# The last part of an encoder's output projection: row tile by row tile, with held-back matmuls, other buffers for its mixer, and another order in the first gates

## Chip, core and metric

The kernel runs on one core of one Trainium2 chip. The metric is the device time of one execution in microseconds (us), the median of several executions. The engines are named as the profile names them: PE is TensorE (matmuls; PEld is its weight load, which overlaps), DVE is VectorE, ACT is ScalarE, POOL is GpSimd, and SP (SyncE) issues the DMAs.

## What is computed

A two-layer encoder over one sequence of 512 tokens of width 1024, in float32. Each layer adds four attention mixers of four heads each (a: a neighbourhood on a grid, b: differential, c: dilated, d: with a latent key and value), projected back by `w_o`, and then a gated feed-forward block; a norm ends the program. Cut to what matters here:

```python
for l in range(DEPTH):
    h = rms_norm(x, attn_norm[l])
    ...
    mix = jnp.concatenate([o_a, o_b, o_c, o_d], axis=-1)
    x = x + mix @ w_o[l]

    h = rms_norm(x, ffn_norm[l])
    x = x + (jax.nn.silu(h @ w_gate[l]) * (h @ w_up[l])) @ w_down[l]
return rms_norm(x, final_norm)
```

## The kernel before

**Products.** Activations lie transposed: 128 channels on the partitions, the 512 tokens along the row. Every float32 operand of a large product is split into a hi part (a cast to fp32r) and a lo part (the rest), and a product is three matmuls, hi by hi, lo by hi and hi by lo. `dense_steps` (L166) writes them for one output tile of 128 by 512: for each of the inputs `k` the weight's hi part by the activation's hi part (L173) and by its lo part (L175), and after all of these the weight's lo part by the activation's hi part (L178). A weight slab of 1024 columns is loaded by SP, cast to hi on ACT (L137; `whi`, two buffers) and subtracted to lo on DVE or POOL (L160; `wlo`, two buffers).

**Order.** Each engine runs its instructions in program order. A scheduler in the framework fixes that order when the program is built, by priorities that follow the order of writing; `tc.issue_after(i)` lets what is written inside stand behind instruction `i`. Attention is written as 56 units of scores (`S_`), transposes (`T_`, tile `tp`) and the product with the values (`V_`, tile `pv`). Between the units, `fill` hands out pieces of dense work at hand-set rates: the input projections, and the output projection in three parts by mixer, `PARTS = ((1,), (2, 3), (0,))`. Part 0 adds mixer b, part 1 mixers c and d (four slabs of two row tiles, `wo1m`), part 2 mixer a (two slabs of four row tiles, `wo2m`). A piece starts when its `gate` is ready. Mixer a is the last to be computed, so part 2 ends the attention of each layer.

**Around the last unit.** `V_` of the last unit (L937) leaves mixer a's last head in the bank `pv`. `fold` copies one half to SBUF on ACT (L137, tile `o`) and adds the other on DVE (L781), and `split` casts the sum to the hi part of tile `mix01` on ACT (L137) and subtracts to its lo part on DVE (L142), each in two pieces. The same has been done for the first two heads (`mix00`). All mixer tiles come from one ring of four buffers, so the tiles of mixer a take those that mixer c's had. `p_out` adds each row tile to the residual `x` on DVE straight from PSUM (L663), or, where the table `ENG` says so (keys `x22`, `x23`, `x27` in part 2), by a copy on ACT (L655) and an add on POOL.

**Into the feed-forward block.** `norm_inputs` makes of each of the eight residual tiles the scaled hi part `h_f` on ACT (L200), the lo part on DVE (L201), and its square on ACT, which POOL adds up (L190, L191). The gate and up slabs of the feed-forward block (tile `gu`) follow, 22 pairs of 24 matmuls a slab, eight inputs in `dense` order.

**The end.** The last output tile is computed in two halves of 256 tokens. For each half a column of `ms` gives the factor `rcol_fin` (POOL), DVE multiplies it into a diagonal (L1154, `dg`), a matmul with ones spreads it over the partitions (L1156, `bc`), and four multiplications on DVE (L1159) and four DMAs end the program.

Of the kernel before, what the change touches and what calls it, by code (L numbers as in the profile page):

```python
# [18 lines left out]
P = 128  # L19
D = 1024  # L20
S = 512
# [17 lines left out]
NEED = {(3, 0, 0): [('out', 0, 1)], (0, 1, 1): [('out', 1, 3)]}  # L39
HEADS = [(1, 0, 0), (1, 0, 1), (1, 1, 0), (1, 1, 1), (2, 0, 0), (2, 0, 1), (2, 1, 0), (2, 1, 1), (3, 0, 0), (3, 0, 1), (3, 1, 0), (3, 1, 1), (0, 0, 0), (0, 0, 1), (0, 1, 0), (0, 1, 1)]  # L40
ORDER = 'f t s 1q1 v2 1k1 2q0 l0 2k0 2k1 l1 kr nq 2q1 nqr l2 nk nkr qr 3r00 3q0 v3 3k1 3q1 v00 3k0 v01 o01 0k0 3r01 3r10 3r11 vt1 0q1 ab 0q0 vt0 0k1 o00 o10 o11 o12 o13 o20 o21'
# [4 lines left out]
ENG = {'b10_l': 'P', 'b11_l': 'P', 'ea00': 'V', 'ea03': 'A', 'ea10': 'A', 'ea13': 'A', 'ec11': 'A', 'ec13': 'A', 'ed00': 'P', 'ed02': 'P', 'ed03': 'A', 'ed11': 'P', 'ed13': 'A', 'fa010': 'P', 'fa110': 'P', 'fa210': 'P', 'fa300': 'P', 'kd_a00': 'P', 'kd_a01': 'V', 'kd_a11': 'P', 'kd_d00': 'P', 'kd_d01': 'P', 'kd_d10': 'P', 'kd_d11': 'P', 'kl_a00': 'P', 'kl_a01': 'P', 'kl_a10': 'P', 'kl_a11': 'P', 'kl_c00': 'P', 'kl_c01': 'P', 'kl_c10': 'P', 'kl_c11': 'P', 'kl_d00': 'P', 'kl_d01': 'P', 'kl_d10': 'P', 'kl_d11': 'P', 'm10_l': 'P', 'm11_l': 'P', 'm20_l': 'P', 'm21_l': 'P', 'm30_l': 'P', 'm31_l': 'P', 'ql_a00': 'P', 'ql_a01': 'P', 'ql_a10': 'P', 'ql_a11': 'P', 'ql_c00': 'P', 'ql_c01': 'P', 'ql_c10': 'P', 'ql_c11': 'P', 'ql_d00': 'P', 'ql_d01': 'P', 'ql_d10': 'P', 'ql_d11': 'P', 'rk2': 'V', 'rq1': 'V', 'sc_ka0': 'P', 'sc_ka1': 'P', 'sc_qn1': 'P', 'wh_ckv': 'V', 'wh_cq0': 'P', 'wh_kb0': 'V', 'wh_qb0': 'V', 'wh_qb1': 'V', 'wh_ud1': 'V', 'wh_ur': 'V', 'wh_vcb': 'V', 'wh_wo00': 'P', 'wh_wo14': 'P', 'wl_qb1': 'V', 'x02': 'P', 'x03': 'P', 'x05': 'P', 'x15': 'P', 'x22': 'P', 'x23': 'P', 'x27': 'P'}  # L46
# [16 lines left out]
def tile_encoder(ctx, tc, xT, gains, lamv, w_in, w_kr, w_d, w_o0, w_o1, w_o2, w_gu, w_dn,  # L63
# [103 lines left out]
    def dense_steps(pt, w, xs, wcol, first=True, last=True):  # L167
# [3 lines left out]
        nk = len(xs)  # L171
        for k in range(nk):
# [20 lines left out]
    def norm_inputs(x, gcol, nm):  # L193
# [3 lines left out]
        for k in range(KD):  # L197
            h = wide(f"h_{nm}{k}", F32R)
            g = gn[:, gcol + k : gcol + k + 1]
            nc.scalar.activation(h[:, 0, :], x(k), AF.Copy, scale=g)  # L200
# [3 lines left out]
            square(acc, x(k), k, nm)  # L204
# [127 lines left out]
    def attention(l, xsrc, x, hs, ssq, pl, nar):  # L332
# [331 lines left out]


        mix = {}

        def mix_tile(m, p):
            if (m, p) not in mix:
                mix[m, p] = pl.tile([P, 2, S], F32R, tag="mix", name=f"mix{m}{p}_{l}", bufs=4)  # L670
            return mix[m, p]
# [649 lines left out]
```

## Time and profile before

| | |
|---|---|
| time, median of 3 executions | 1305.89 us (1305.41 to 1307.08) |
| the profiled execution's own time | 1306.79 us |
| its span, first to last instruction | 1305.0 us |
| PE busy | 1275.5 us, 98% of the span |
| DVE, ACT, POOL busy | 687.6, 588.8, 474.9 us |
| mean granted clock of PE over the span | 0.994 |

The profiled execution lies 0.90 us above the median; 1.8 us of its time lie outside the span. The granted clock is given as a share of 2.4 GHz: 1.00 is that level, 0.50 the lower one of 1.2 GHz, and a value between them is a stretch with some of both. A row of the view by stretches tells, for each engine, in the order PE, PEld, DVE, ACT, POOL, how long it was busy in the stretch and how many of its instructions lie in it (one on an edge may count on both sides). A matmul's record is longer than its share of PE's time, since one drains while the next runs; what it costs is the distance from its start to the next start.

### The profile page before, as it was taken

What the parts mean: (1) busy time and instruction counts of PE and PEld (TensorE: products, weight loads), DVE (VectorE), ACT (ScalarE), POOL (GpSimd) and SP (SyncE); (2) the same over time, 40 slices, a digit from 0 to 9 for tenths busy, and PEclk for the clock granted to TensorE, in tenths of its full rate; (3) what the DMA queues carried; (4) which work ended last, traced back from release to release, by engine and by line L of the source; (5) the groups of instructions that cost most, each with busy time, mean ns of one, the idle gap of its engine ahead of it and who ended that gap; (6) DMA issues with size and microseconds to landing.
All of it is one profiled execution on the core that took longest, in us unless ns stands there. A gap on an engine that the chain in (4) does not pass through costs nothing. (4 is left out here: it accounts for less than half of the span.)

```text
span 1305.0 us, 17103 instructions
## 1 busy us (share of the span) xinstructions
PE 1275.5 (98%) x6362; PEld 1067.1 (82%) x6362; DVE 687.6 (53%) x1168; ACT 588.8 (45%) x1022; POOL 474.9 (36%) x371
## 2 busy tenths in 40 slices
PE   8999999999999999999999999999899999999997
PEld 8788888877888888888898788888688888888886
DVE  6588756665444444323237787565654444442232
ACT  5376866753333333222316777676433333333230
POOL 1276685763111111100246469656521111110000
PEclk9999999989999999999999999999999999999998
DMA  5552441112222222333346333311222222233221
GB/s 191 175 166 85 134 118 65 67 64 97 97 97 97 97 97 93 101 118 107 122 129 176 111 103 111 122 65 66 75 87 97 97 97 97 97 93 101 89 89 65
DMA packets 50915, 135.63 MB, mean 104 GB/s; under 512 B 7896, under 2 KB 12760, under 8 KB 50832
## 3 DMA queue, kind: packets, MB, share of 16 engines
q1 hardware_dynamic: 50544, 134.25, 32.3%
q8 instruction: 50, 0.82, 0.3%
q10 hardware_dynamic: 288, 0.29, 0.1%
q14 instruction: 33, 0.27, 0.1%
HBM read 119.01 MB, written 4.23 MB: 94 GB/s over the span
## 5 line engine op out<-in xcount | busy, mean ns | idle before, releaser
L175 PE MATMUL gu<-h_f,whi_gu 128*128 128x512 f32 x704 | 274.3, 390 | 1.5 <-DVE h_f L201 1.5
L173 PE MATMUL gu<-h_f,whi_gu 128*128 128x512 f32 x704 | 274.0, 390 | 0.1
L1110 POOL TENSOR_TENSOR u<-u,th 128x512 f32<-128x512 f32 x44 | 93.2, 2118 | 367.6 <-DVE u L1108 351.5
L178 PE MATMUL gu<-h_f,wlo_gu 128*128 128x512 f32 x704 | 173.9, 389 | 0.0
L175 PEld LDWEIGHTS gu<-h_f,whi_gu 128*128 128x128 f32 x704 | 132.0, 188 | 31.0 <-DVE h_f L201 4.0
L173 PEld LDWEIGHTS gu<-h_f,whi_gu 128*128 128x128 f32 x704 | 132.2, 188 | 28.3 <-DVE x L663 1.0
L178 PEld LDWEIGHTS gu<-h_f,wlo_gu 128*128 128x128 f32 x704 | 132.1, 188 | 27.4
L137 ACT CAST whi_gu<-raw_gu 128x1024 fp32r<-128x1024 f32 x88 | 92.7, 1054 | 105.5 <-PE gu L175 104.9
L173 PE MATMUL dn<-act,whi_dn 128*128 128x512 f32 x330 | 128.4, 389 | 0.0
L175 PE MATMUL dn<-act,whi_dn 128*128 128x512 f32 x330 | 128.4, 389 | 0.0
L160 DVE TENSOR_TENSOR wlo_gu<-raw_gu,whi_gu 128x1024 fp32r<-128x1024 f32 x88 | 110.4, 1255 | 20.3 <-ACT whi_gu L137 18.7
L692 ACT ACTIVATE e<-e,mx 128x512 f32<-128x512 f32 (+1 forms) x128 | 85.5, 669 | 49.0 <-DVE mx L690 44.3
L160 DVE TENSOR_TENSOR wlo_dn<-raw_dn,whi_dn 128x1024 fp32r<-128x1024 f32 (+1 forms) x45 | 51.1, 1135 | 100.4 <-PE dn L178 61.0
L137 ACT CAST whi_dn<-raw_dn 128x1024 fp32r<-128x1024 f32 (+1 forms) x45 | 44.2, 982 | 127.7 <-PE dn L175 111.2
L137 ACT CAST act<-u 128x512 fp32r<-128x512 f32 x44 | 27.3, 620 | 155.1 <-POOL u L1110 155.1
L1108 DVE SCALAR_TENSOR_TENSOR u<-gu,bc_ff 128x512 f32<-128x512 f32 x44 | 30.4, 691 | 122.8 <-PE gu L178 122.8
L142 DVE TENSOR_TENSOR tl<-tp,th 128x512 fp32r<-128x512 f32 x112 | 75.6, 685 | 28.7 <-ACT th L137 28.0
L178 PE MATMUL dn<-act,wlo_dn 128*128 128x512 f32 x330 | 82.1, 389 | 0.0
L690 DVE CUSTOM_DVE_ANT_0 e<-sc,t 128x512 f32<-128x512 f32 x96 | 65.0, 684 | 32.3 <-PE tp L853 12.6
L178 PEld LDWEIGHTS dn<-act,wlo_dn 128*128 128x128 f32 x330 | 61.9, 188 | 12.9
L175 PEld LDWEIGHTS dn<-act,whi_dn 128*128 128x128 f32 x330 | 61.9, 188 | 12.9
L173 PEld LDWEIGHTS dn<-act,whi_dn 128*128 128x128 f32 x330 | 61.9, 188 | 12.8
(484 smaller groups left out, 2644.6 us busy)
## 6 DMA issues: line engine op xcount, KB each, us to landing
raw_gu<-in_w_gu_dram SPq DMA_DIRECT2D x88, 512.0 KB, 3.2
raw_dn<-in_w_dn_dram SPq DMA_DIRECT2D x32, 512.0 KB, 3.5
raw_wo<-in_w_o_dram SPq DMA_DIRECT2D x16, 512.0 KB, 3.5
t<-tb SPq DMA_DIRECT2D x16, 448.0 KB, 4.1
raw_dn<-in_w_dn_dram SPq DMA_DIRECT2D x16, 384.0 KB, 3.0
sb<-kbn SPq DMA_DIRECT2D x64, 64.0 KB, 2.0
sb<-qbn SPq DMA_DIRECT2D x64, 64.0 KB, 2.0
xin<-in_xT_dram SPq DMA_DIRECT2D x8, 256.0 KB, 5.6
```

What stands on the lines that cost most here:

```text
L137: nc.scalar.copy(out, src)
L142: engine(tag, usual).tensor_tensor(out, src, hi.bitcast(F32), op=ALU.subtract)
L160: lo_eng.tensor_tensor(lo[:, c], raw[:, c], hi[:, c].bitcast(F32), op=ALU.subtract)
L173: nc.tensor.matmul(pt, whi[:, k, wcol], xs[k][:, 0, :], start=first and k == 0, stop=False)
L175: nc.tensor.matmul(pt, whi[:, k, wcol], xs[k][:, 1, :], start=False, stop=False)
L178: nc.tensor.matmul(pt, wlo[:, k, wcol], xs[k][:, 0, :], start=False, stop=last and k == nk - 1)
L690: nc.vector.tensor_tensor_reduce(out=e, in0=sc, in1=bias, scale=1.0, scalar=BIG, op0=ALU.add, op1=ALU.min, accum_out=mx)
L692: nc.scalar.activation(e, src, AF.Exp, bias=mx, scale=-1.0, accum_out=den)
L1108: nc.vector.scalar_tensor_tensor(u, pts[1], 0.5, r_bc, op0=ALU.mult, op1=ALU.mult)
L1110: nc.gpsimd.tensor_tensor(u, u, th, op=ALU.mult)
```

## The change

- In part 1 the last slab (`wo16`, `wo17`) waits for a new mark, `last`, which the transposes of the last unit set; from then on `fill` places the work behind the last unit's `pv` matmuls, whose last one is now the unit's mark.
- Part 2 is one piece, `p_out_last`: both slabs are asked for at its start, its row tiles cycle through the four banks of `acc` and `sc`, each row tile does its six matmuls tile of the mixer by tile of the mixer (hi by hi, hi by lo, lo by hi), each row tile stands behind the one before, and every add to `x` is on DVE from PSUM. `ENG` loses its keys `x22`, `x23` and `x27`.
- The tiles of mixer a come from the ring `st` of ten buffers.
- `norm_inputs` of the feed-forward block writes the squares behind the last hi part.
- The first gate and up slab (`m == 0`) take all hi by hi matmuls first, then the weight's lo part, and the activation's lo part last.
- At the end two transposes of the factor's column (L1195) take the place of the diagonal and the matmul with ones.

```diff
-NEED = {(3, 0, 0): [('out', 0, 1)], (0, 1, 1): [('out', 1, 3)]}
+NEED = {(3, 0, 0): [('out', 0, 1)], (0, 1, 1): [('out', 1, 2)]}
...
+        if lo_last:
+            for i, (w, a) in enumerate(((whi, 0), (wlo, 0), (whi, 1))):
+                for k in range(nk):
+                    nc.tensor.matmul(pt, w[:, k, wcol], xs[k][:, a, :], start=first and i + k == 0,
+                                     stop=last and i == 2 and k == nk - 1)
+                    yield 1.0
+            return
...
-            square(acc, x(k), k, nm)
+            if not late:
+                square(acc, x(k), k, nm)
+        if late:
+            with tc.issue_after(last.ins):
+                for k in range(KD):
+                    square(acc, x(k), k, nm)
...
+        def p_out_last(part, kts):
+            xs = [mix[k] for k in kts]
+            ws = []
+            for i in range(2):
+                w = slab((w_o0, w_o1, w_o2)[part][l][:, i * SLAB : (i + 1) * SLAB], SLAB, nc.gpsimd, f"wo{part}{4 * i}{l}")
+                ws.append(tuple(t.rearrange("p (m k c) -> p m k c", m=4, k=2) for t in w))
+            last = None
+            for m in range(KD):
+                pt = ps.tile([P, 512], F32, tag=("acc", "sc")[m // 2 % 2], name=f"wo{part}{m}{l}", bufs=2)
+                with tc.issue_after(last.ins) if last else ExitStack():
+                    for k in range(2):
+                        whi, wlo = (t[:, m % 4, k] for t in ws[m // 4])
+                        nc.tensor.matmul(pt, whi, xs[k][:, 0, :], start=k == 0, stop=False)
+                        nc.tensor.matmul(pt, whi, xs[k][:, 1, :], start=False, stop=False)
+                        last = nc.tensor.matmul(pt, wlo, xs[k][:, 0, :], start=False, stop=k == 1)
+                nc.vector.tensor_tensor(x(m), x(m), pt, op=ALU.add)
+            yield 48.0
...
-                mix[m, p] = pl.tile([P, 2, S], F32R, tag="mix", name=f"mix{m}{p}_{l}", bufs=4)
+                mix[m, p] = st_tile(f"mix{m}{p}") if m == 0 else pl.tile(
+                    [P, 2, S], F32R, tag="mix", name=f"mix{m}{p}_{l}", bufs=4)
...
+                if p and hh:
+                    ready.add("last")
...
-                    key=("out", part, i // n), gate=[(m, p) for m in ms for p in range(2)])
+                    key=("out", part, i // n),
+                    gate=[(m, p) for m in ms for p in range(2)] + ["last"] * (part == 1 and i + n == KD))
...
             i = now[0] - PACE
+            if "last" in ready:
+                i = len(units) - 1
...
-                dense(pt, w, hs, slice(0, P))
+                dense(pt, w, hs, slice(0, P), lo_last=m == 0)
...
-            dg = pl.tile([P, 2, P], F32, tag="dg", name=f"dg{h}", bufs=2)
-            nc.vector.tensor_tensor(dg, ident.unsqueeze(1).to_broadcast([P, 2, P]),
-                                    r[:, :2].unsqueeze(2).to_broadcast([P, 2, P]), op=ALU.mult)
-            marks[h, 2] = nc.tensor.matmul(b1[:, :256], ones, dg.rearrange("p a b -> p (a b)"), start=True, stop=True)
+            for c in range(2):
+                marks[h, 2] = nc.tensor.transpose(b1[:, c * P : (c + 1) * P], r[:, c : c + 1].to_broadcast([P, P]), ident)
...
-        hs, ssq = norm_inputs(x, G_FFN + KD * l, f"f{l}")
+        hs, ssq = norm_inputs(x, G_FFN + KD * l, f"f{l}", True)
```

How the instructions move is shown for the first layer; the second layer moves alike, and outside these places and the end of the program each engine's order stays as it was.

**PE around the last unit's `pv`.** `wo16m` is a row tile of part 1 (`wo160` is row tile 6 in layer 0), `wo200` and `wo210` are row tiles 0 and 1 of part 2, `mix2..` and `mix3..` are mixers c and d, `mix00` and `mix01` mixer a. Before:

```order
L178 MATMUL wo170_3134<-mix31_0_2934,wlo_wo160_3116 128x512
L937 MATMUL pv_01110_3266<-th_01110_3250,v_a0_2314 128x2x128
L937 MATMUL pv_01110_3266<-tl_01110_3251,v_a0_2314 128x2x128
...
L173 MATMUL wo200_3289<-mix00_0_3215,whi_wo200_3284 128x512
L173 MATMUL wo210_3297<-mix00_0_3215,whi_wo200_3284 128x512
L175 MATMUL wo200_3289<-mix00_0_3215,whi_wo200_3284 128x512
L175 MATMUL wo210_3297<-mix00_0_3215,whi_wo200_3284 128x512
L173 MATMUL wo200_3289<-mix01_0_3277,whi_wo200_3284 128x512
```

After:

```order
L183 MATMUL wo160_3238<-mix31_0_2934,whi_wo160_3233 128x512
L973 MATMUL pv_01110_3247<-th_01110_3215,v_a0_2314 128x2x128
L973 MATMUL pv_01110_3247<-tl_01110_3216,v_a0_2314 128x2x128
...
L186 MATMUL wo160_3238<-mix20_0_2090,wlo_wo160_3234 128x512
...
L181 MATMUL wo170_3268<-mix20_0_2090,whi_wo160_3233 128x512
...
L186 MATMUL wo170_3268<-mix31_0_2934,wlo_wo160_3234 128x512
L691 MATMUL wo200_3296<-mix00_0_3180,whi_wo200_3284 128x512
L692 MATMUL wo200_3296<-mix00_0_3180,whi_wo200_3284 128x512
L693 MATMUL wo200_3296<-mix00_0_3180,wlo_wo200_3285 128x512
L691 MATMUL wo200_3296<-mix01_0_3258,whi_wo200_3284 128x512
```

Sixteen of the 24 matmuls of part 1's last slab (the four lo matmuls of row tile 6 and the twelve of row tile 7) moved from ahead of the eight `pv` matmuls to behind them, and three matmuls with `mix00` now stand ahead of the first one with `mix01`; the slab's other eight stay ahead of `pv`.

**DVE around the last `fold`.** `tl` is the lo part of the transposed probabilities, `o01` the folded sum of mixer a's second pair of heads, `x03` holds residual tiles 6 and 7. Before:

```order
L663 TENSOR_TENSOR x03_2037<-x03_2037,wo160_3120 128x512
L142 TENSOR_TENSOR tl_01110_3251<-tp_011100_3252,th_01110_3250 128x512
L142 TENSOR_TENSOR tl_01110_3251<-tp_011101_3259,th_01110_3250 128x512
L663 TENSOR_TENSOR x03_2037<-x03_2037,wo170_3134 128x512
L142 TENSOR_TENSOR mix00_0_3215<-o00_0_3062,mix00_0_3215 128x3x8x16
L142 TENSOR_TENSOR mix00_0_3215<-o00_0_3062,mix00_0_3215 128x8x2x8
L781 TENSOR_TENSOR o01_0_3245<-o01_0_3245,pv_01110_3266 64x512
L142 TENSOR_TENSOR mix01_0_3277<-o01_0_3245,mix01_0_3277 128x3x8x16
```

After:

```order
L142 TENSOR_TENSOR mix00_0_3180<-o00_0_3062,mix00_0_3180 128x3x8x16
L142 TENSOR_TENSOR mix00_0_3180<-o00_0_3062,mix00_0_3180 128x8x2x8
L676 TENSOR_TENSOR x01_2878<-x01_2878,wo130_3050 128x512
L142 TENSOR_TENSOR tl_01010_3186<-tp_010100_3187,th_01010_3185 128x512
L142 TENSOR_TENSOR tl_01010_3186<-tp_010101_3194,th_01010_3185 128x512
L676 TENSOR_TENSOR x02_2007<-x02_2007,wo140_3083 128x512
L142 TENSOR_TENSOR tl_01110_3216<-tp_011100_3217,th_01110_3215 128x512
L142 TENSOR_TENSOR tl_01110_3216<-tp_011101_3224,th_01110_3215 128x512
L815 TENSOR_TENSOR o01_0_3210<-o01_0_3210,pv_01110_3247 64x512
L676 TENSOR_TENSOR x03_2037<-x03_2037,wo160_3238 128x512
L142 TENSOR_TENSOR mix01_0_3258<-o01_0_3210,mix01_0_3258 128x3x8x16
```

The two subtractions for `mix00` went from just ahead of the last `fold` to the place behind the fold of their own pair, ahead of the `tl` of the last two units.

**ACT from the first hi part to the third gate slab.** `h_f0k` is the scaled hi part of residual tile k, `sq_f0k` its square, `whi_gu000` and `whi_gu010` the first gate and up slab, `whi_gu100` the next gate slab. Before:

```order
L200 ACTIVATE h_f04_3391<-x02_2007,gn_73 128x512
L200 ACTIVATE h_f05_3397<-x02_2007,gn_73 128x512
L190 ACTIVATE sq_f04_3394<-x02_2007 128x512
L137 CAST whi_gu010_3467<-raw_gu010_3465 128x1024
L200 ACTIVATE h_f06_3403<-x03_2037,gn_73 128x512
L655 COPY po27_0_3363<-wo270_3356 128x512
L190 ACTIVATE sq_f05_3400<-x02_2007 128x512
L190 ACTIVATE sq_f06_3406<-x03_2037 128x512
L200 ACTIVATE h_f07_3409<-x03_2037,gn_73 128x512
L190 ACTIVATE sq_f07_3412<-x03_2037 128x512
L137 CAST whi_gu100_3509<-raw_gu100_3507 128x1024
```

After:

```order
L137 CAST whi_gu010_3461<-raw_gu010_3459 128x1024
L208 ACTIVATE h_f06_3381<-x03_2037,gn_73 128x512
L208 ACTIVATE h_f07_3384<-x03_2037,gn_73 128x512
L195 ACTIVATE ssq_f0_3362<-x00_2855 128x512
L198 ACTIVATE sq_f01_3388<-x00_2855 128x512
L198 ACTIVATE sq_f02_3391<-x01_2878 128x512
L198 ACTIVATE sq_f03_3394<-x01_2878 128x512
L198 ACTIVATE sq_f04_3397<-x02_2007 128x512
L198 ACTIVATE sq_f05_3400<-x02_2007 128x512
L198 ACTIVATE sq_f06_3403<-x03_2037 128x512
L137 CAST whi_gu100_3503<-raw_gu100_3501 128x1024
```

All eight squares now stand behind the last hi part, seven of them ahead of the cast of the third slab.

## Rows read from the trace of the kernel before

**Rows 1.** PE's waits over the span: us in total, times, longest us.

```profile
PE wo L175 <- DVE mix L142: 3.4, 2, 1.7
...
PE bc L1156 <- DVE dg L1154: 1.5, 1, 1.5
PE gu L175 <- DVE h_f L201: 1.5, 4, 0.5
```

**Rows 2.** View by stretches: us, busy us (instructions) by engine, PEclk, DMA, GB/s.

```profile
263.93:271.12 7.19, 7.19 (x41) 6.01 (x39) 2.82 (x5) 3.90 (x7) 5.02 (x5) 1.00 0.21 73
271.12:275.07 3.95, 1.46 (x5) 0.59 (x4) 3.29 (x4) 1.29 (x3) 2.23 (x2) 0.91 0.15 43
275.07:281.20 6.13, 6.12 (x14) 4.75 (x15) 3.34 (x6) 2.49 (x4) 0.26 (x1) 0.50 0.15 58
281.20:288.74 7.54, 7.45 (x31) 5.22 (x29) 5.29 (x7) 6.14 (x10) 7.01 (x5) 1.00 0.19 70
288.74:301.39 12.65, 11.92 (x48) 8.89 (x49) 9.60 (x6) 6.67 (x10) 9.27 (x6) 1.00 0.13 43
...
313.69:319.13 5.44, 5.44 (x25) 4.50 (x24) 4.21 (x4) 2.30 (x3) 2.44 (x2) 1.00 0.26 96
...
912.42:916.38 3.96, 1.46 (x5) 0.59 (x5) 3.30 (x4) 1.29 (x3) 2.24 (x2) 0.96 0.16 46
916.38:919.74 3.36, 3.36 (x8) 2.56 (x9) 1.23 (x3) 0.10 (x1) 0.00 (x0) 0.54 0.26 102
919.74:929.82 10.08, 9.19 (x37) 6.29 (x37) 8.45 (x10) 8.30 (x14) 7.64 (x5) 1.00 0.16 52
929.82:942.47 12.65, 11.91 (x48) 8.89 (x49) 9.61 (x6) 6.67 (x10) 9.27 (x6) 1.00 0.12 41
```

**Rows 3.** Timelines at layer 0's last fold: start, us, engine, instruction, idle before.

```profile
270.53 2.83 POOL L160 TENSOR_TENSOR wlo_wo<-raw_wo,whi_wo 128x512 fp32r<-128x512 f32 x2 [2.17 <-ACT whi_wo L137]
...
270.90 2.60 DVE L142 TENSOR_TENSOR mix<-o,mix 128x384 fp32r<-128x384 f32 x2
273.53 0.69 DVE L781 TENSOR_TENSOR o<-o,pv 64x512 f32<-64x512 f32 x1
274.86 0.76 DVE L142 TENSOR_TENSOR mix<-o,mix 128x384 fp32r<-128x384 f32 x2 [0.63 <-ACT mix L137]
...
271.23 0.58 ACT L137 COPY o<-pv 64x512 f32<-64x512 f32 x1 [0.16 <-PE pv L937]
274.31 0.71 ACT L137 CAST mix<-o 128x384 fp32r<-128x384 f32 x2 [2.51 <-DVE o L781]
```

**Rows 4.** Timelines ahead of layer 0's last `pv`.

```profile
263.80 0.38 PE L924 MATMUL tp<-ident,e 128*128 128x128 f32 x2
...
264.59 0.58 ACT L784 COPY oh<-pv 64x512 f32<-64x512 f32 x1
267.07 1.07 ACT L137 CAST th<-tp 128x512 fp32r<-128x512 f32 x2 [1.90 <-PE tp L924]
...
267.69 1.29 DVE L142 TENSOR_TENSOR tl<-tp,th 128x512 fp32r<-128x512 f32 x2
```

**Rows 5.** Squares' adds and lo parts (min/median/max ns); a slab's cast.

```profile
L191 POOL TENSOR_TENSOR ssq_f<-ssq_f,sq_f x14: 1332/1624/2272, 280.9 to 937.7; 128x512 f32<-128x512 f32 x14
...
L201 DVE SCALAR_TENSOR_TENSOR h_f<-x,gn,h_f x16: 748/1184/1781, 279.5 to 936.4; 128x512 fp32r<-128x512 f32 x16
...
297.71 1.05 ACT L137 CAST whi_gu<-raw_gu 128x1024 fp32r<-128x1024 f32 x1 [2.17 <-PE gu L175]
```

**Rows 6.** Timeline of the program's end; PE's transposes of layer 0's norm factors.

```profile
1296.70 0.70 POOL L252 TENSOR_TENSOR rcol_fin<-col_fin,mhalf 128x2 f32<-128x2 f32 x1 [6.88 <-DVE col_fin L250]
...
1297.91 0.84 PE L1156 MATMUL bc<-dg,ones 128*128 128x256 f32 x2 [1.49 <-DVE dg L1154]
1298.79 2.48 DVE L1159 TENSOR_TENSOR x<-x,bc 128x512 f32<-128x512 f32 x4 [0.93 <-PE bc L1156]
...
308.24 0.60 PE L266 MATMUL rows_ff<-ident,rcol_ff 128*128 128x128 f32 x4
```

## What the change was predicted to do

> **What bounds the kernel now.** The table of busy times comes first: PE is busy for 98% of the span, so a change can only pay where PE waits, runs at the lower clock or does other work. The change neither adds nor removes large matmuls. The next view is PE's list of waits. Three of its entries belong to the code that the change touches, all of them single waits once or twice a layer [rows 1]: the first matmuls of part 2 wait for the mixer's lo part (3.4 us in two waits), the end waits for the diagonal (1.5 us), the first gate for lo parts of `h_f` (1.5 us in four waits). The third view, by stretches, shows what the list hides: behind the wait for the mixer the granted clock falls, to 0.50 for the 6.13 us from 275.07 in layer 0 and to 0.54 for 3.36 us in layer 1 [rows 2]. That is the lower level of 1.2 GHz, after PE had worked for 1.46 of 3.95 us.
>
> What these stretches would take without waits comes from a slab of 24 matmuls in the steady feed-forward block: 5.44 us at 1.00, or 0.227 us each [rows 2]. Part 2 has 48 matmuls, which fall into the stretches as 4, 14 and 30 in layer 0 and as 4, 8 and 36 in layer 1; the two slabs of the first gate have 48 more. The loss of each stretch is its length less its matmuls at 0.227 us:
> Layer 0: hand-over 3.95 − 0.91 = 3.04; lower clock 6.13 − 3.18 = 2.95; rest of part 2 7.54 − 6.81 = 0.73; first gate 12.65 − 10.90 = 1.75. Sum 8.47 us.
> Layer 1: 3.96 − 0.91 = 3.05; 3.36 − 1.82 = 1.54; 10.08 − 8.17 = 1.91; 12.65 − 10.90 = 1.75. Sum 8.25 us.
> So 16.7 us can be had at these two places, and no more.
>
> **The hand-over, and what is late next.** In layer 0 the chain runs from ACT's copy of `pv` at 271.23 to the end of ACT's cast of `mix01` at 275.02, 3.8 us [rows 3]. Of these, DVE stands for 2.60 us on the two subtractions for `mix00`, which take 0.76 us for `mix01` a little later; POOL's subtraction of a weight slab (2.83 us) lies beside the slow pair [rows 3]. The change takes the slow pair out of the chain (the other ring lets it run when its own heads are done, on a DVE that then has gaps), which leaves copy 0.58, add 0.69, cast 0.71: 2.0 us, some 2.4 with hand-offs, and 0.76 more for the lo part. Meanwhile PE now has 16 held-back matmuls and three with `mix00`: 19 × 0.227 = 4.3 us. Even the old chain of 3.8 us would nearly fit. I cost this wait at nothing, and without it see no reason for the clock to fall.
>
> What is given for it: the same 16 matmuls no longer stand between the last transposes and `pv`. The transposes now stand together from 263.80, about 0.5 us, and eight matmuls follow (1.9 us), so PE reaches `pv` at about 266.3. ACT ends its copy `oh` at 265.17 and then casts `th`; the lo parts end 1.91 us behind that cast's start in the trace (267.07 to 268.98), so now at about 267.05 [rows 4]. The fourth `pv` matmul waits for that, and the last starts 0.4 us later than without a wait. Price 0.4 us a layer, between 0 (transposes slower by that much) and 1.0 (one more ACT instruction of 0.6 us ahead of the cast).
>
> **Part 2 row tile by row tile.** PE then goes from about 267.7 through 16 + 48 matmuls, 14.5 us, and ends part 2 at about 282.2. A row tile lasts 6 × 0.227 = 1.36 us; its add on DVE takes 0.69 us from PSUM, and the `h_f` lo part 0.75 us at best, 1.18 at the median [rows 3, 5]. DVE keeps up at 0.75 and runs a few tenths a tile late at 1.18; since four banks cycle and the gate wants the lo parts last, 0.4 us a tile harm nobody. The three adds that leave POOL and the three copies that leave ACT cost PE nothing, and POOL falls silent there.
>
> **The first gate.** Twelve hi by hi matmuls need only `h_f00` to `h_f05` and both weight casts. The second slab's buffer comes free with the last row tile, at 282.2; its cast (1.05 us [rows 5]) ends at about 283.3, and six matmuls (1.36 us) cover it to 283.6. This is tight by 0.3 us. The lo parts are wanted from about 288, when DVE has been through them. I take this stretch's 1.75 us as won.
>
> **The third slab.** Here the change adds a wait. ACT now does all eight squares behind the last hi part, and the cast of the third slab is queued behind seven of them. The ring of squares has two buffers, so the seventh square waits for POOL's fourth add. ACT is through the hi parts at about 284.8, through two squares at 286.0; with an add of `a` us the cast is done at 286.0 + 4a + 0.6 + 1.05. PE wants it at 282.3 + 10.9 = 293.2. POOL's adds took 1.33 at least, 1.62 at the median, 2.27 at most [rows 5]; the cast is then ready at 293.0, 294.1 or 296.7, and PE waits 0, 0.9 or 3.5 us. The fast adds are those with little on DVE beside them, and DVE has nothing left from about 287.5. I take 1.45 us, near the fast end: 0.3 us of wait, and 0.4 us for small hand-offs. The Trainium skill, page "SBUF — State Buffer", section "Who interferes with whom", says that a DVE instruction with two SBUF inputs and a GpSimd instruction that reads SBUF exclude each other for a whole instruction, and that no other pair of engines does. This case's slow pair beside POOL agrees (2.60 against 0.76 us); by that rule the adds run at 1.33 us, the wait is 0 and the time 0.6 us lower.
>
> **The end.** From the end of `rcol_fin` at 1297.40 to the first multiplication at 1298.79 lie 1.39 us: diagonal, two matmuls of 0.84 us, hand-offs [rows 6]. Now two transposes stand there; four took 0.60 us at the full level [rows 6], so two take 0.3 to 0.6 us with hand-offs, twice that at the lower level. Gain 0.3 to 1.0 us; I take 0.8, as PE has just worked at 1.00.
>
> **The sum.** New waits a layer: 0.4 + 0.3 + 0.4 = 1.1 us. Gain: (8.47 − 1.1) + (8.25 − 1.1) + 0.8 = 15.3 us. The profiled execution took 1306.79 us, so 1291.5 us; it lies 0.90 us above the median, and so does the forecast: **1290.6 us**. With no new wait and the best end the gain is 16.7 + 1.0 = 17.7, or 1288.2. With 1.0, 3.5 and 0.5 us of new waits a layer it is 16.7 − 10.0 + 0.3 = 7.0, or 1298.9.
>
> **Rivals.**
> *The third slab is late and the clock falls there.* The wait is 2 to 3.5 us, as long as the one that lowered the clock before. For: the hi parts and the squares of eight tiles are now one queue on ACT. Against: DVE's silence. At adds of 1.9 us (the middle of median and slowest) the wait is 2.1 us, 1.8 more than forecast, and a fall costs what it cost before (2.95 and 1.54): 1290.6 + 3.6 + 4.5 = 1298.7 us.
> *The hold does not cover.* The chain behind `pv` grows again (ACT's queue, POOL's `o` add), PE idles before `mix01` and the clock falls as now: the first two terms of each layer are lost, 10.6 us, 1301.2 us. It also covers the case that the change does not do what it says; the order of instructions speaks against that.
> *Slower: the clock falls in the row tiles.* Part 2 now changes banks every six matmuls and waits at `pv`. If the clock falls at `pv` and these short groups don't raise it, every matmul costs 0.438 − 0.227 = 0.21 us more (14 in 6.13 us [rows 2]). With all 48 of part 2 in both layers this is 20.2 us: 1310.8. It decides from 15.3/0.21 = 73 matmuls on, 36 a layer. Against: the 30 matmuls from 281.20, in groups of six too, ran at 1.00 [rows 2]. The Trainium skill, page "TensorE: Matmul & The Clock Gate", section "A second HAM failure mode: psum-queue depth-cycling", tells of a kernel whose cycling through banks left PE so many short pauses that the clock swung; this row does not bear it out here.
>
> **How the numbers follow.** A measurement of this kernel can tell about 0.2%, 2.6 us, from no change. Forecast 0.75; late third slab 0.14; no cover 0.04; no change from something unseen 0.03; slower 0.04. The range from 1288.0 to 1297.0 holds the forecast with its bounds but the very worst, and the milder half of the late slab; the other half, the cases without cover, without change and slower make 0.18. Faster is forecast, late slab and no cover: 0.93.
>
> **What the profile will show.** Right: in PE's waits no wait for `mix` over 0.3 us, one of about 0.4 us at the last `pv` a layer; granted clock 1.00 through both part 2s; the third slab begins near 293 in layer 0 and near 927 in layer 1 (layer 0's 8 us earlier than before, layer 1's 15.5 us); at the end under 0.8 us from `rcol_fin` to the first multiplication. Wrong: a wait of PE for ACT's `whi_gu` behind squares, a granted clock below 1.00 at either place, or DVE a whole row tile behind in part 2.

## The result, and the profile after

| | before | changed |
|---|---|---|
| time, median | 1305.65 us (1305.37 to 1307.08) | 1289.89 us (1289.56 to 1290.48) |
| the profiled execution's own time | 1306.79 us | 1289.56 us |
| span | 1305.0 us | 1287.7 us |

The ratio is 0.9878, with a 95% interval from 0.9861 to 0.9895: 15.8 us are gone (before has four executions here, one more than in the first table). Forecast were 1290.6 us and a range from 1288.0 to 1297.0.

The busy times of the changed kernel, at the head of its page:

```profile
span 1287.7 us, 17099 instructions
## 1 busy us (share of the span) xinstructions
PE 1268.1 (98%) x6362; PEld 1067.2 (83%) x6362; DVE 678.9 (53%) x1172; ACT 586.0 (46%) x1016; POOL 458.7 (36%) x365
```

PE has as many instructions as before and is busy for 7.4 us less: most of that is the stretches at the lower clock. The rest of the gain was idle time. PE's waits, in us in total, times, longest:

```profile
PE pv L900 <- DVE tl L142: 2.0, 5, 0.5
...
PE bc L1195 <- POOL rcol_fin L265: 1.0, 1, 1.0
```

None of the three entries of [rows 1] is left, but for the end's, which went from 1.5 to 1.0 us. The view by stretches, with the columns of [rows 2], shows what they left behind. The stretches are: in layer 0 the last transposes and `pv`, the 16 held matmuls, part 2, the first gate; in layer 1 the last three of these:

```profile
263.44:267.38 3.94, 3.85 (x26) 3.28 (x25) 1.29 (x2) 2.13 (x4) 3.94 (x4) 1.00 0.18 65
267.38:271.03 3.65, 3.65 (x18) 3.01 (x17) 2.05 (x4) 2.00 (x4) 0.61 (x1) 1.00 0.19 73
271.03:281.91 10.88, 10.88 (x49) 9.01 (x48) 9.31 (x14) 5.54 (x8) 2.54 (x2) 1.00 0.27 96
281.91:292.91 11.00, 11.00 (x49) 8.80 (x47) 4.10 (x7) 7.37 (x12) 7.10 (x6) 1.00 0.16 49
900.28:903.92 3.64, 3.64 (x19) 3.01 (x17) 2.06 (x4) 2.00 (x4) 0.63 (x1) 1.00 0.25 95
903.92:914.80 10.88, 10.88 (x50) 9.01 (x48) 9.32 (x14) 5.54 (x8) 2.54 (x2) 1.00 0.29 96
914.80:925.81 11.01, 11.01 (x50) 8.80 (x48) 4.10 (x7) 7.38 (x12) 7.11 (x6) 1.00 0.14 48
```

Part 2 takes 10.88 us, its 48 matmuls at 0.227 us and nothing besides; the granted clock is 1.00 throughout. The first gate has 48 matmuls in 11.00 us, 0.1 more than it needs.

**Where the 17.3 us of span went.** Matching matmuls of the two traces by name, the changed kernel is 0.36 us ahead before the last transposes of layer 0 (263.80 before, 263.44 after), 8.34 us ahead in the rest of layer 0, 8.74 us ahead before the last unit of layer 1, 16.51 us after it and 17.3 us at the end. So layer 0's transition gave 8.34 − 0.36 = 7.98 us of the 8.47 that could be had, layer 1's 16.51 − 8.74 = 7.77 of 8.25, the end 0.8. The remaining 0.36 + 0.40 = 0.76 us lie in attention, in stages that the change doesn't touch; such leads come and go between executions (last section).

### The profile page after: what moved, and what is told of

The parts are those of the page before. It is cut to its first block, busy times and chain, and to the rows that moved or that the text cites. A ratio compares the mean times of both kernels' runs of the same rounds, so it can differ in the third digit from the quotient of the medians.

```text
span 1287.7 us, 17099 instructions
## 1 busy us (share of the span) xinstructions
PE 1268.1 (98%) x6362; PEld 1067.2 (83%) x6362; DVE 678.9 (53%) x1172; ACT 586.0 (46%) x1016; POOL 458.7 (36%) x365
## 4 chain that ended last, share of the span: by engine, by line
PE 88%; DVE 5%; DMA 2%; issue 2%; ACT 2%; SPq 1%; POOL 0%; POOLq 0%; DVEq 0%; ACTq 0%
PE gu L181 12%; PE gu L183 12%; PE gu L186 12%; PE dn L186 6%; PE dn L181 6%; PE dn L183 6%; PE tp L887 2%; PE wo L186 2%; PE gu L176 2%; PE wo L183 2%; PE wo L181 1%; PE pv L900 1%; PE pv L899 1%; DVE tl L142 1%; PE sc L396 1%
## 5 line engine op out<-in xcount | busy, mean ns | idle before, releaser
L181 PE MATMUL gu<-h_f,whi_gu 128*128 128x512 f32 x672 | 261.9, 390 | 0.0
L183 PE MATMUL gu<-h_f,whi_gu 128*128 128x512 f32 x672 | 261.7, 389 | 0.0
L1151 POOL TENSOR_TENSOR u<-u,th 128x512 f32<-128x512 f32 x44 | 90.3, 2053 | 358.2 <-DVE u L1149 339.2
L186 PE MATMUL gu<-h_f,wlo_gu 128*128 128x512 f32 x672 | 166.0, 389 | 0.0
L181 PEld LDWEIGHTS gu<-h_f,whi_gu 128*128 128x128 f32 x672 | 126.1, 188 | 26.8 <-ACT whi_gu L137 0.7
L186 PEld LDWEIGHTS gu<-h_f,wlo_gu 128*128 128x128 f32 x672 | 126.1, 188 | 26.2
L183 PEld LDWEIGHTS gu<-h_f,whi_gu 128*128 128x128 f32 x672 | 126.2, 188 | 26.1
```

Source lines behind the costliest of these rows:

```text
L181: nc.tensor.matmul(pt, whi[:, k, wcol], xs[k][:, 0, :], start=first and k == 0, stop=False)
L183: nc.tensor.matmul(pt, whi[:, k, wcol], xs[k][:, 1, :], start=False, stop=False)
L186: nc.tensor.matmul(pt, wlo[:, k, wcol], xs[k][:, 0, :], start=False, stop=last and k == nk - 1)
L1151: nc.gpsimd.tensor_tensor(u, u, th, op=ALU.mult)
```

## Experiments

Each kernel below is the changed one or the one before with one edit. The ratio is to the kernel before, timed beside it. The next columns come from the traces and are us lost by PE at the two places, layer 0 / layer 1: from the start of the last `pv` matmul to the first gate matmul, less the matmuls between at 0.227 us (64 where 16 are held, 48 before, 45 in `e1_no_hold` and 46 in `e8_before_ring`, where the first ones with `mix00` go ahead of `pv`); and the two first gate slabs less 10.90 us (and less 0.81 where the eight `ms_ff` matmuls stand among them).

| kernel | median us | ratio, 95% interval | to the gate | gate |
|---|---|---|---|---|
| before | 1305.65 | 1 | 6.9 / 6.7 | 1.75 / 1.75 |
| changed | 1289.89 | 0.9878 (0.9861 to 0.9895) | 0.1 / 0.1 | 0.1 / 0.1 |
| `changed_again` | 1288.95 | 0.9875 (0.9860 to 0.9889) | 0.1 / 0.1 | 0.1 / 0.1 |
| `e1_no_hold` | 1298.37 | 0.9935 (0.9916 to 0.9955) | 4.6 / 4.6 | 0.0 / 0.1 |
| `e2_old_ring` | 1300.32 | 0.9954 (0.9937 to 0.9971) | 5.1 / 4.9 | 0.1 / 0.1 |
| `e8_before_ring` | 1301.43 | 0.9958 (0.9944 to 0.9972) | 4.5 / 4.5 | 1.75 / 1.75 |
| `e9_before_hold` | 1306.74 | 0.9999 (0.9990 to 1.0009) | 5.5 / 7.0 | 1.75 / 1.75 |
| `e3_lo_in_pairs` | 1290.88 | 0.9871 (0.9854 to 0.9887) | 0.1 / 0.1 | 0.0 / 0.0 |
| `e4_squares_between` | 1294.58 | 0.9904 (0.9886 to 0.9922) | 0.1 / 0.1 | 2.2 / 2.2 |
| `e6_two_pieces` | 1294.03 | 0.9891 (0.9872 to 0.9910) | 1.1 / 1.1 | 0.6 / 0.7 |
| `e11_before_squares` | 1301.91 | 0.9969 (0.9958 to 0.9979) | 4.9 / 7.0 | 0.1 / 0.1 |
| `e7_late_slab` | 1289.89 | 0.9865 (0.9850 to 0.9880) | 0.1 / 0.1 | 0.1 / 0.1 |
| `e10_late_slab` | 1297.73 | 0.9936 (0.9923 to 0.9949) | 0.1 / 0.1 | 2.8 / 2.8 |
| `e5_old_end` | 1291.97 | 0.9894 (0.9881 to 0.9908) | 0.1 / 0.1 | 0.1 / 0.1 |

The changed kernel itself was timed once more, beside `e5_old_end`, `e10_late_slab` and `e11_before_squares`:

> The changed kernel once more, as the mark against which the three others of this call and the small differences are read: 1289.9 us, ratio to the kernel before near 0.988.

It took 1288.95 us, with nearly the same ratio as the first time (0.9875).

### The hand-over: hold, ring, or both

Two kernels take one of the two edits out of the changed kernel, two put one into the kernel before. Without the hold:

```diff
-                    gate=[(m, p) for m in ms for p in range(2)] + ["last"] * (part == 1 and i + n == KD))
+                    gate=[(m, p) for m in ms for p in range(2)])
...
-            if "last" in ready:
-                i = len(units) - 1
```

> The changed kernel without the hold: part 1's last slab runs ahead of the last pv again, all else as changed. Nothing now stands between the last pv and mix01, so PE should wait for copy 0.58, add 0.69 and cast 0.71 us plus hand-offs, and for the lo part after that: 2.4 us a layer. Theory (a wait of this length lowers the clock there, as in the kernel before): 2 x 2.4 + 2.95 + 1.54 = 9.3 us over the changed kernel's 1289.9, 1299.2 us, granted clock near 0.5 for some us behind the wait. Rival (the shorter wait lets the clock stand): 4.8 us, 1294.7 us, clock 1.00.

It took 1298.37 us. PE's wait, and layer 0's stretches of the wait and behind it:

```profile
PE wo L691 <- ACT mix L137: 4.4, 2, 2.2
```

```profile
272.44:274.79 2.35, 0.16 (x2) 0.00 (x0) 0.91 (x2) 1.29 (x3) 1.33 (x2) 1.00 0.07 9
274.79:278.91 4.12, 4.01 (x9) 2.96 (x10) 1.99 (x4) 0.72 (x1) 0.00 (x0) 0.59 0.33 122
```

The wait of 2.2 us is the chain of copy, add and cast, and behind it the clock is at 0.59 for 4.1 us, in layer 1 at 0.73. The theory held: the hold is worth what it covers and the clock besides.

With the old ring for mixer a's tiles:

```diff
-                mix[m, p] = st_tile(f"mix{m}{p}") if m == 0 else pl.tile(
+                mix[m, p] = pl.tile(
                     [P, 2, S], F32R, tag="mix", name=f"mix{m}{p}_{l}", bufs=4)
```

> The changed kernel with mixer a's tiles back in the old ring of four. Theory from the prediction (16 held matmuls and three with mix00 are 4.3 us, the old chain was 3.8, so the hold alone nearly covers): within 0.5 us of 1289.9. Rival (the hold needs the ring: mix00 takes the tile of a mixer that the held matmuls still read, so its cast can start only when the last of them is done, near 270.4 in layer 0, behind a weight cast of 1.05 us): PE waits for mix00's hi part, its lo part and mix01 one after the other, 2.1 to 4.0 us a layer, without or with a fall of the clock (up to 4.5 us in both layers): 1294 to 1302, 1299 us as a middle.

It took 1300.32 us: 0.8% behind the changed kernel by the ratios, which is no better than without the hold (the two intervals overlap). The theory from the prediction fell, and the rival held. Its timelines (start, us, engine, instruction, idle before):

```profile
270.43 1.05 ACT L137 CAST whi_wo<-raw_wo 128x1024 fp32r<-128x1024 f32 x1 [2.21 <-PE wo L183]
271.39 1.32 ACT L137 CAST mix<-o 128x384 fp32r<-128x384 f32 x4
271.93 3.27 DVE L142 TENSOR_TENSOR mix<-o,mix 128x384 fp32r<-128x384 f32 x4
271.56 2.81 POOL L160 TENSOR_TENSOR wlo_wo<-raw_wo,whi_wo 128x512 fp32r<-128x512 f32 x2 [3.50 <-ACT whi_wo L137]
```

`mix00` takes a tile that the held matmuls still read. Its casts start when these are through, at 271.4, behind a weight cast on ACT (270.43 to 271.48) that had itself waited for the held matmuls; in the changed kernel the casts of `mix01` (from 268.97) stand ahead of that weight cast (from 270.32). Both mixer tiles are then made in a row, the first pair on DVE beside POOL's subtraction again. The sixteen matmuls cover only the copy and the add; the casts and the subtractions begin when they end. PE waits 0.9 us for the hi part and 1.9 us for the lo part.

The two single edits on the kernel before say the same. The ring alone:

```diff
-                mix[m, p] = pl.tile([P, 2, S], F32R, tag="mix", name=f"mix{m}{p}_{l}", bufs=4)
+                mix[m, p] = st_tile(f"mix{m}{p}") if m == 0 else pl.tile(
+                    [P, 2, S], F32R, tag="mix", name=f"mix{m}{p}_{l}", bufs=4)
```

> The kernel before with one edit, mixer a's tiles in the ring of ten. The slow pair of subtractions (2.60 us) leaves the chain. Theory: PE's wait shrinks from 3.0 to about 2.4 us a layer and the clock still falls behind it: 1305.7 - 1.2 = 1304.5 us. Rival: the chain was all that mattered and the shorter wait leaves the clock at 1.00: 1305.7 - 1.2 - 4.5 = 1300 us.

1301.43 us, 5.5 us faster by the ratio (3.7 to 7.3): nearer the rival. For the mixer PE waits once, 1.7 us a layer in place of 2.5, and in the profiled execution the clock stayed (0.998 over the span; the five others have 0.993 to 0.997, which does not tell where it fell). A second wait, 0.8 us for an add to `x` on DVE, now comes in both layers; the kernel before has it in one:

```profile
PE wo L173 <- ACT mix L137: 3.5, 2, 1.7
```

```profile
271.84:274.19 2.35, 0.62 (x4) 0.19 (x2) 0.91 (x2) 1.29 (x3) 1.57 (x2) 1.00 0.00 0
274.19:280.00 5.81, 5.71 (x23) 4.02 (x24) 3.42 (x6) 3.49 (x6) 1.03 (x1) 1.00 0.26 90
```

The hold alone (the gate and the two lines of `fill` from the first diff above put into the kernel before, with the marks that they need and the changed entry of `NEED`):

> The kernel before with one edit, 16 matmuls of part 1's last slab held behind the last pv. Theory from the prediction (the hold covers the chain by itself): PE waits at most 0.5 us a layer, the clock stands, 1305.7 - 2 x 2.6 - 4.5 = 1296 us. Rival (the old ring ties mix00 to the held matmuls, so the chain only begins when the cover is used up): the wait stays 2 to 4 us a layer, the clock falls as before, 1303 to 1308 us, no measurable gain.

1306.74 us, ratio 0.9999: nothing. Its waits are those of the kernel before:

```profile
PE wo L175 <- DVE mix L142: 3.4, 2, 1.7
...
PE wo L173 <- ACT mix L137: 1.8, 2, 0.9
```

So hold and ring are not two savings. The ring alone takes 2.3 us a layer off the way to the gate, the hold alone nothing that can be measured, and together they take all but 0.1, with part 2's new form, and all but 1.1 with its old one (`e6_two_pieces`, next).

### Part 2 and the first gate

Part 2 in its two old pieces (`o20 o21` in `ORDER`, `PARTS` whole, `x22`, `x23`, `x27` back in `ENG`):

> The changed kernel with part 2 in its two old pieces (two banks, three of the eight adds by a copy on ACT and an add on POOL), hold and ring as changed. Theory A (POOL's add makes row tile 7 some 1.2 us later, the squares start later by as much, and the third slab's cast has no slack): 0.3 to 1.5 us a layer, 1.3 taken: 1292.5 us. Rival B (hold and ring carry the whole hand-over, part 2's form is worth nothing): 1289.9 us. Rival C (part 2 loses what its rest lost before, 0.73 and 1.91 us): 1292.5 us, but then with waits of PE for x or a bank inside part 2 rather than at the gate slabs.

By the traces it loses 1.0 us more a layer to the gate and 0.5 more in it, 3.0 us together; the medians differ by 4.1, the ratios by 1.7 with intervals that overlap. B fell. C has the larger part: 1.0 us goes in short pauses of part 2 and before the gate, of which the view of waits names only one of 0.3 us for DVE's add. Of A the cause came true and the path did not. POOL's add makes the last hi part late, and PE waits for that hi part, which with the slow start behind the wait is the 0.5 us. The squares come later too, but the third slab's cast stands behind six of them here, and ends at 295.38 for a PE that starts the slab at 296.53:

```profile
285.95 1.93 POOL L676 TENSOR_TENSOR x<-x,po 128x512 f32<-128x512 f32 x1 [4.09 <-ACT po L668]
286.65 1.77 DVE L209 SCALAR_TENSOR_TENSOR h_f<-x,gn,h_f 128x512 fp32r<-128x512 f32 x1
287.91 0.72 ACT L208 ACTIVATE h_f<-x,gn 128x512 fp32r<-128x512 f32 x1 [1.42 <-POOL x L676]
...
288.69 0.50 PE L176 MATMUL gu<-h_f,whi_gu 128*128 128x512 f32 x1 [0.21 <-ACT h_f L208]
```

The order inside the first gate:

```diff
-                dense(pt, w, hs, slice(0, P), lo_last=m == 0)
+                dense(pt, w, hs, slice(0, P))
```

> The changed kernel with the first gate's matmuls in the old order, hi and lo part of each input in turn, the weight's lo part last. Theory A (DVE now ends the lo parts in time but for the last two): from the changed kernel's trace the lo parts 6 and 7 of h_f end at 285.3 and 286.0 in layer 0, where PE would want them at 284.9 and 285.3; the wait is 0.7 us a layer, of which 0.1 was the third slab's: 1289.9 + 1.2 = 1291.1 us. Rival B (the stretch costs what it cost before, 1.75 us a layer): 1289.9 + 3.5 = 1293.4 us.

Neither held. The ratio is 0.9871, no difference, and the gate takes 10.88 us:

```profile
283.50:294.38 10.88, 10.88 (x50) 9.01 (x48) 5.44 (x7) 8.14 (x12) 7.05 (x5) 1.00 0.13 50
```

Theory A reckoned as if the first slab ran through before the second; the program's order then mixes the two slabs, and the pairs of inputs 6 and 7 come late enough. What pays is that the lo parts are early. That is the squares' doing:

```diff
-        hs, ssq = norm_inputs(x, G_FFN + KD * l, f"f{l}", True)
+        hs, ssq = norm_inputs(x, G_FFN + KD * l, f"f{l}")
```

> The changed kernel with each square written behind its own hi part instead of all behind the last. Theory A (ACT then has 0.73 + 0.62 us a row tile against PE's 1.36, and two casts of 1.05 us besides, so the last hi parts come about 1.5 us later than now, near 285.8 where PE wants them near 284.6): 1 us a layer more, 1291.9 us. Rival B (the third slab's cast comes earlier and nothing else is late): 0.1 us a layer less, 1289.7 us, no measurable difference.

It took 1294.58 us, with 2.1 us a layer more at the gate: twice theory A's 1 us, and for the first of two waits by another path than ACT's own queue. PE waits 0.5 us for a hi part and 1.0 us for the second slab's cast, which stands behind hi parts and squares on ACT. Ahead of that hi part ACT had been idle for 2.4 us, waiting for DVE's add to `x`:

```profile
285.14 0.72 ACT L208 ACTIVATE h_f<-x,gn 128x512 fp32r<-128x512 f32 x1 [2.44 <-DVE x L694]
```

Grouped by operation over 274 to 294 us, first the changed kernel with the squares between, then (273 to 288, POOL's 281 to 293) the changed one (busy us, mean ns):

```profile
L209 DVE SCALAR_TENSOR_TENSOR h_f<-x,gn,h_f 128x512 fp32r<-128x512 f32 x8 | 10.0, 1265 | 0.0
L694 DVE TENSOR_TENSOR x<-x,wo 128x512 f32<-128x512 f32 x8 | 5.4, 681 | 1.4 <-PE wo L693 1.3
L199 POOL TENSOR_TENSOR ssq_f<-ssq_f,sq_f 128x512 f32<-128x512 f32 x7 | 12.2, 1737 | 3.9 <-ACT sq_f L198 3.6
```

```profile
L209 DVE SCALAR_TENSOR_TENSOR h_f<-x,gn,h_f 128x512 fp32r<-128x512 f32 x8 | 5.9, 746 | 0.0
L694 DVE TENSOR_TENSOR x<-x,wo 128x512 f32<-128x512 f32 x8 | 5.4, 684 | 1.4 <-PE wo L693 1.3
L199 POOL TENSOR_TENSOR ssq_f<-ssq_f,sq_f 128x512 f32<-128x512 f32 x6 | 8.2, 1366 | 11.8 <-ACT sq_f L198 11.4
```

Beside POOL's adds a lo part takes 1265 ns on the mean, without them 746, and POOL's add 1737 for 1366; the adds to `x` that read PSUM take 0.68 us in both. It is POOL and not ACT's squares that stretch the lo parts: in `e6_two_pieces` one takes 1.77 us beside POOL's add to `x` (the row from 286.65 above), before ACT begins any square. With the extra 4.1 us on DVE the adds to `x` come late, and ACT's hi parts after them.

The other way round, the late squares alone in the kernel before:

> The kernel before with one edit, the feed-forward block's squares behind the last hi part. Theory A (the stretch of the first gate, 1.75 us a layer, was DVE's lo parts slowed by POOL's adds and ACT's squares, not the order of the gate's matmuls): 2 x 1.75 = 3.5 us less than the kernel before, the two gate slabs in 10.9 us where they took 12.65. Rival B (the order of the gate's matmuls is what pays): no more than 1 us less, the gate's lo parts still late by 0.5 us a time. The hand-over keeps its wait and its lower clock by both.

1301.91 us, 4.0 us less by the ratio (2.7 to 5.5). Theory A held: with the old order of its matmuls the gate takes 11.01 us where [rows 2] have 12.65.

```profile
286.19:297.20 11.01, 11.01 (x48) 9.12 (x49) 5.97 (x5) 7.99 (x13) 7.86 (x6) 1.00 0.15 49
```

### The third slab, and the end

To see whether the third slab's cast has room, POOL's work ahead of it was lengthened:

```diff
+        twice = nm in ("f0", "f1") and k in (1, 2)
-        nc.scalar.activation(sq, xk, AF.Square)
+        nc.scalar.activation(sq, xk, AF.Square, scale=0.5**0.5 if twice else 1.0)
-        nc.gpsimd.tensor_tensor(acc, acc, sq, op=ALU.add)
+        for _ in range(1 + twice):
+            nc.gpsimd.tensor_tensor(acc, acc, sq, op=ALU.add)
```

> The changed kernel with the second and the third square scaled by one half and added twice by POOL: two more adds of 1.37 us stand ahead of the seventh square, and so ahead of the cast of the third slab. Theory A (the cast sits on the edge, every further us is PE's): PE waits 2.7 us more for that cast in each layer, 1289.9 + 5.4 = 1295.3 us with the clock at 1.00. Rival B (such a wait also lowers the clock, as at the old hand-over): up to 4.5 us more, 1299.8 us. Rival C (there is slack that the trace does not show): 1289.9 to 1291 us.

1289.89 us and no new wait, which looked like rival C. It was not a test: the scheduler put the cast ahead of the sixth square, so that five stood ahead of it in place of seven, and it ended at 292.57 for a PE that started the slab at 292.63. With the cast kept behind the seventh square by `tc.issue_after`:

> The changed kernel with the second and third square scaled by one half and added twice by POOL, and now the cast of the third slab kept behind the seventh square, where it stands in the changed kernel. Theory A (the cast sits on the edge): PE waits 2.7 us more for it in each layer, 1289.9 + 5.4 = 1295.3 us, clock 1.00. Rival B (such a wait also lowers the clock, as at the old hand-over in some layers and executions): up to 4.5 us more, 1299.8 us. Rival C (slack that the trace does not show): 1289.9 to 1291 us.

1297.73 us. This lies between A's 1295.3 and B's 1299.8. The wait is there in both layers, 2.6 us each:

```profile
PE gu L182 <- ACT whi_gu L137: 5.3, 2, 2.6
```

So there is no room behind the cast (theory A). The clock fell behind the wait in one of the two layers (last section).

The end as it was (the diagonal and the matmul with ones in place of the two transposes):

> The changed kernel with the old end: diagonal on DVE and one matmul with ones in place of the two transposes. Prediction: 0.8 us more than the changed kernel; by the changed kernel's own trace, from the end of rcol_fin to the first multiplication, 0.79 us for 1.39, it is 0.6 us, 1290.5 us. Rival (the first half's diagonal delays PE in the last output tile as well): 0.8 to 1.0 us more.

It took 1291.97 us, 3.0 more than `changed_again`. From the end of `rcol_fin` to the first multiplication the old end took 1.25 us here (1283.81 to 1285.06), at a granted clock of 0.99. The changed one, in these rows of its trace, took 0.79 (1280.66 to 1281.45):

```profile
1279.97 0.69 POOL L265 TENSOR_TENSOR rcol_fin<-col_fin,mhalf 128x2 f32<-128x2 f32 x1 [6.66 <-DVE col_fin L263]
...
1280.72 0.69 PE L1195 MATMUL bc<-ident,rcol_fin 128*128 128x128 f32 x2 [1.03 <-POOL rcol_fin L265]
1281.45 2.48 DVE L1198 TENSOR_TENSOR x<-x,bc 128x512 f32<-128x512 f32 x4 [1.55 <-PE bc L1195]
```

But there the granted clock was 0.50. In `changed_again` it was 0.90 over the same stretch, which took 0.52 us (1280.00 to 1280.52):

```profile
1280.05 0.43 PE L1195 MATMUL bc<-ident,rcol_fin 128*128 128x128 f32 x2 [1.03 <-POOL rcol_fin L265]
1280.52 2.48 DVE L1198 TENSOR_TENSOR x<-x,bc 128x512 f32<-128x512 f32 x4 [1.30 <-PE bc L1195]
```

So at nearly the same clock the last chain is worth 0.7 us. With 0.2 us for the first half's matmul, which no longer stands among PE's, the end is worth 0.9 us, the rival's figure. Matching the traces of this kernel and of `changed_again`, 3.6 us more were lost before 1260 us, in code that is the same in both: 1.8 us by 146 us, among them a wait of 0.9 us for `v_d`, and 2.0 us in layer 1's attention, less a start that was 0.3 us ahead. The time of this kernel therefore neither bears out nor denies 0.9 us; the traces do.

## Why the prediction was right, point by point

**Bound, losses and the sum.** The losses read from [rows 2], 8.47 and 8.25 us, were there to be had, and 7.98 and 7.77 were. New waits were forecast at 1.1 us a layer and measured at 0.5. The forecast gain of 15.3 us on the profiled execution was 17.2 there: 2 × 0.6 too much for new waits, and 0.8 from leads in attention. The median hides part of that: the profiled execution of before lies 1.1 us above its median, that of after 0.3 below. That the median came within 0.7 us of the forecast is in part luck; by the profiled execution the forecast was 1.9 us too high.

**The hand-over.** No wait for `mix`: right. The reason was half wrong. "Even the old chain of 3.8 us would nearly fit" under the held matmuls is refuted by `e2_old_ring` and `e9_before_hold`: in the old ring the casts of the chain can't start until the held matmuls, readers of their tile, are done, and PE waited 0.9 and 1.9 us a layer in the first, 0.9 and 1.7 in the second. The step that failed is the one that laid chain and cover side by side without asking from where the chain may begin. The forecast stood because both edits are in the change.

**The wait at `pv`.** Forecast for the fourth `pv` matmul, 0.4 us. It came at the fourth:

```profile
266.30 0.28 PE L973 MATMUL pv<-th,v_a 128*128 128x256 f32 x1
266.68 0.38 PE L973 MATMUL pv<-tl,v_a 128*128 128x256 f32 x1
266.90 0.28 PE L973 MATMUL pv<-th,v_a 128*128 128x256 f32 x1
```

0.38 us between starts where 0.12 is the rule: 0.26 us, in both layers.

**Part 2.** 10.88 us at 1.00. DVE is busy for 9.31 of it, as forecast late by less than a tile (its adds start at most 1.1 us after the last matmul of their row tile, which lasts 1.36), and nobody waits. The lo parts took 746 ns, the best end of [rows 5].

**The first gate.** Won, as forecast, but the change's reason there was not weighed: the new order of the matmuls is worth nothing once the squares are late (`e3_lo_in_pairs`), and the late squares alone bring the gate from 12.65 to 11.01 us (`e11_before_squares`). The prediction took the squares for a cost only.

**The third slab.** Forecast 0.3 us, measured 0.1, and by the forecast chain:

```profile
283.59 0.71 ACT L208 ACTIVATE h_f<-x,gn 128x512 fp32r<-128x512 f32 x1
284.21 0.62 ACT L195 ACTIVATE ssq_f<-x 128x512 f32<-128x512 f32 x1
284.73 1.14 ACT L198 ACTIVATE sq_f<-x 128x512 f32<-128x512 f32 x2
...
291.29 0.63 ACT L198 ACTIVATE sq_f<-x 128x512 f32<-128x512 f32 x1 [0.74 <-POOL ssq_f L199]
291.83 1.04 ACT L137 CAST whi_gu<-raw_gu 128x1024 fp32r<-128x1024 f32 x1
```

The cast ends at 292.87, PE starts the slab at 292.91 and could have at 292.8. Two terms cancelled in part. ACT was through the hi parts at 284.30, not 284.8, and through the first two squares, which POOL's first add needs, at 285.34, not 286.0; so POOL's chain starts at 285.42, 0.6 us earlier. And PE was 0.4 us earlier than 293.2. The term for the adds was right: from 285.42 to 291.26 the four adds ahead of the seventh square took 1.46 us each with their hand-offs, and 1.45 was taken. The first, which starts beside DVE's last lo part, lasted 1.72 us, each of the others 1.29. The rule of the Trainium skill (page "SBUF — State Buffer", section "Who interferes with whom"), from which the prediction had drawn adds of 1.33 us and no wait, came nearer for the wait, and fits the three adds that had nothing on DVE beside them. `e4_squares_between` agrees with it in kind: DVE's lo parts, two inputs in SBUF, go from 746 to 1265 ns beside POOL's adds, DVE's adds with one input in PSUM stay at 0.68 us.

**The end.** Forecast were 0.8 us, by the traces of before and changed it was 0.6 on the last chain and 0.2 in the first half. That the sum fits is luck: the forecast counted the last chain alone, with PE at 1.00. The clock was at 0.50 there, and the first half, which the forecast left out, made up for it.

**The rivals.** The late third slab is real as a mechanism, and `e10_late_slab` prices it: 2.6 us of wait a layer, 8.0 us by the ratios of the kernels timed together, clock included. "The hold does not cover" is what the change would have been without its ring, 1300.3 us against 1301.2 worked out. The clock fell in none of the row tiles, in the two profiled executions of the changed kernel.

## What to carry over

When work is held back to cover a chain, look up which buffers the held work still reads: if the chain writes into one of them, that part of it starts when the cover ends, and the hold brings nothing until the ring is changed as well. Two edits that each seem to pay for the same stall have to be tried alone and together. And a side job on ACT and POOL (here the squares) may cost its time on DVE: moving it behind the work that PE waits for was worth more than another order of the matmuls.

## What was not expected of the hardware

**The same wait does not always lower the clock.** The prediction counted the lower clock behind the old hand-over, 2.95 and 1.54 us, as lost each time. `e9_before_hold` has the same two waits (0.9 and 1.7 us) in both layers of one execution. The wait and the 6.1 us behind it, layer 0 and layer 1:

```profile
268.60:276.08 7.48, 4.88 (x22) 3.41 (x20) 5.01 (x7) 2.85 (x6) 3.44 (x3) 1.00 0.10 38
276.08:282.20 6.12, 6.02 (x26) 4.46 (x25) 3.15 (x6) 3.81 (x7) 1.36 (x2) 1.00 0.25 86
908.53:916.02 7.49, 4.90 (x21) 3.47 (x20) 5.02 (x7) 2.85 (x6) 3.43 (x3) 0.98 0.11 42
916.02:922.13 6.11, 6.11 (x20) 4.59 (x20) 2.85 (x6) 2.35 (x5) 0.00 (x0) 0.75 0.24 86
```

26 instructions against 20 in the same time, 1.00 against 0.75. `e10_late_slab`, behind a single wait of 2.63 us, has it the other way round; the 3.1 us behind the wait:

```profile
294.91:298.03 3.12, 3.12 (x7) 2.49 (x8) 3.12 (x2) 1.43 (x2) 2.61 (x2) 0.51 0.00 0
...
933.61:936.73 3.12, 3.12 (x14) 2.59 (x15) 3.12 (x2) 1.43 (x2) 2.62 (x2) 1.00 0.03 5
```

Over the profiled executions of `before`, `e1`, `e2`, `e8`, `e9`, `e10` and `e11`, the clock fell behind 9 of 14 such waits, of 1.7 to 2.8 us in all, and behind none of the changed kernel's waits of 0.26 us at `pv`. What decides between two equal waits these runs don't show. So the clock's share of the gain, 4.5 us in the profiled execution of before, is what one execution paid; in the next it may be less. The range of `e10_late_slab`, with such a wait (1294.62 to 1299.95 us in six executions), is wider than that of the changed kernel (1288.56 to 1290.55 in eight), but `e3_lo_in_pairs`, without one, also spans 3.2 us.

**Such falls also come in untouched stages.** The view by stretches of the changed kernel's first 40 us, and of `e5_old_end` in layer 1's attention:

```profile
20.00:40.00 20.00, 18.28 (x96) 14.71 (x94) 10.93 (x29) 5.03 (x11) 3.52 (x3) 0.91 0.36 107
```

```profile
740.00:760.00 20.00, 17.55 (x88) 14.38 (x89) 18.71 (x41) 12.60 (x28) 15.94 (x13) 0.91 0.26 78
```

With waits in attention, such as the 0.9 us for `v_d`, they make the leads of 1 to 2 us by which executions of nearly the same program differ, and are why differences under some 2 us were read from the stretches and not from the medians here.
